# A decoder block on one core: the first adaLN vectors through TensorE, six blocks in step, constants loaded after them

## The chip, the core and the metric

The kernel runs on one core of one Trainium2 chip. The metric is device microseconds for one execution of the whole program, from the profiler's side the span from the first to the last instruction plus a little around it. Before the change three runs took 2737.02, 2737.36 and 2742.2 us; the median, 2737.36 us, is the time that a change is compared with. Engines are named as the profile names them: PE is the matrix engine, PEld its weight loads, DVE the vector engine, ACT the scalar engine, POOL GpSimd, SP the engine that issues all the DMAs here.

## The reference

One decoder layer, batch 1, 2048 tokens, width 1024, all float32. A condition vector gives six vectors of 1024; the first two shift and scale the input of the token-mixing sub-layer, the others come later:

```python
cond = jax.nn.silu(c)
mod = (cond @ w_ada[l] + b_ada[l])[:, None, :]
sh1, sc1, g1, sh2, sc2, g2 = jnp.split(mod, N_MOD, axis=-1)
h = rms_norm(x, norm1_g[l]) * (1 + sc1) + sh1
proj = h @ w_in[l]
gq, gk, gv, gr, glr, aq, ak, av = jnp.split(proj, split_at, axis=-1)
# gated linear attention on the first five, dilated attention on the last three
x = x + g1 * (mixed @ w_out[l])
h = rms_norm(x, norm2_g[l]) * (1 + sc2) + sh2
u = causal_depthwise_conv(h @ w_up[l], conv_w[l], conv_b[l])
x = x + g2 * ((jax.nn.silu(u_gate) * u_val) @ w_down[l])
```

`w_ada` is 1024 x 6144 floats, 25 MB: 48 row blocks of 128 outputs, 512 KB each. Blocks 0 to 7 give sh1 and 8 to 15 sc1.

## The kernel before

Tokens go through in four chunks of 512, channels on the partitions. A float32 product is made of three matmuls in a faster format: each operand is split into a high part (a cast on ACT, `hhi` for activations, `whi` for weights) and the remainder (a subtraction on DVE, or on POOL where `pool=True`: `hlo`, `wlo`), and `mm3` adds high x high, high x low and low x high into PSUM. A weight block is loaded into one of two `wraw` buffers and split into one of three `whi`/`wlo` pairs (`wslot`, `wblock`).

**The start** (`run`, up to `self.consts()`). `ada_setup` loads the condition, broadcast over the partitions, and makes the SiLU; `load_x` loads chunk 0; `norm_stats` makes the RMS factor. Then a loop over the eight channel blocks k: `ada(8 + k)` and `ada(k)` load two 512 KB row blocks of `w_ada` (already transposed, so that the outputs lie on the partitions), and DVE multiplies each with the broadcast condition and sums along the row in one instruction (`tensor_tensor_reduce`, in the profile CUSTOM_DVE_ANT_0, line 281). `norm_mod1` then scales and shifts block k of x (line 331 on DVE, 333 on ACT, 335 on DVE) into `hhi` and `hlo`. Four blocks of the input projection (`FIRST`, 128 columns of `w_ch` each) have their weights ready and take each k as it comes.

**After the start** `consts()` loads the constant tables, masks, convolution weights and norm gains; only the table itself waits (`after`) for the seventh turn of the loop (`GATE`), the other loads go as early as the scheduler puts them. The rest of the 32 row blocks of `w_ada` (g1, sc2, sh2, g2) follow one after another through ONE buffer (`tag="v4", bufs=1`): the load of the next can be issued only when DVE has finished with the one before. In program order these 32 steps are laid along the 52 steps of the input projections (`along` in `run`). `proj(0)` finishes chunk 0: four blocks gq, gk out of the four that `FIRST` has made, then the token-major blocks (`tok`, 272 or 256 columns, x as the stationary operand) and the eight q and k blocks (`qk`); `begin(1)` prepares chunk 1's `hhi` and `hlo`, whose squares are summed by `norm_stats` before.

**What sets the order.** The program text gives the order of dependencies; a scheduler then places every instruction on its engine by its own model of durations. Each engine, and SP for the loads, works its list strictly from the top. From the second quarter of the list on, the lists of before and of the change are nearly the same; they differ at the start.

## Time and profile before

| | before |
|---|---|
| median of 3 runs | 2737.36 us |
| profiled execution, its time | 2739.4 us |
| its span, mean granted clock | 2737.6 us, 0.978 |
| PE busy over the span | 2622.8 us (96%) |
| DVE, ACT, POOL busy | 1889.6, 1265.5, 518.8 us |
| bytes moved | 405.19 MB |

The profiled execution took 2.0 us more than the median of the runs. Busy PE does not mean PE at its peak, because matmuls overlap: a matmul's record lasts about 0.39 us where the next starts 0.23 us behind it. Rows of the timeline give the start (us from the span's start), the duration, the engine, the line, the operation and its operands; what stands in square brackets is the idle time before and what ended it.

### The profile page before, as it was taken

The numbers are of one execution on the slowest core, as the hardware profiler recorded it, in microseconds if no ns is written. First come the engines' busy times: TensorE is split into PE (matmuls) and PEld (weight loads), VectorE is DVE, ScalarE is ACT, GpSimd is POOL, SyncE is SP. The second block draws the span as 40 slices with busy tenths as digits, with TensorE's granted clock in tenths as the row PEclk, the third lists the DMA queues.
The fourth block names the chain that finished last, engine by engine and source line by source line (L and its number), as shares of the span: only waits on it lengthen the run. The fifth ranks groups of instructions, "written<-read, shape, count | busy, mean of one in ns | idle before, by whom it ended". The sixth has DMA issues, their size and how long they took to land.

```text
span 2737.6 us, 48297 instructions
## 1 busy us (share of the span) xinstructions
PE 2622.8 (96%) x18920; PEld 2172.7 (79%) x18920; DVE 1889.6 (69%) x3740; ACT 1265.5 (46%) x2606; POOL 518.8 (19%) x324
## 2 busy tenths in 40 slices
PE   5989999999979999999999999999999999999999
PEld 4978888888858887778777888887777788788887
DVE  8777575555567776667987677778877667575655
ACT  3555456465435444443544444435444444343332
POOL 1233242222222211100230111013111100011110
PEclk9999999999979999999999999999999999999999
DMA  7877454554632333336434444544443435333232
GB/s 276 289 260 243 145 186 154 195 173 147 197 113 93 99 123 122 106 122 232 137 97 124 130 136 126 169 168 128 130 129 113 140 122 187 125 100 100 93 100 93
DMA packets 196230, 405.19 MB, mean 148 GB/s; under 512 B 19474, under 2 KB 78627, under 8 KB 194723
## 3 DMA queue, kind: packets, MB, share of 16 engines
q1 hardware_dynamic: 196002, 402.11, 45.1%
q8 instruction: 149, 2.44, 0.4%
q14 instruction: 79, 0.64, 0.1%
HBM read 339.12 MB, written 62.91 MB: 147 GB/s over the span
## 4 chain that ended last, share of the span: by engine, by line
PE 66%; DVE 14%; ACT 9%; DMA 7%; issue 3%; SPq 1%; POOL 0%; DVEq 0%; ACTq 0%; POOLq 0%
PE psg L239 19%; PE psg L241 19%; PE psg L240 19%; DMA wada<-in_w_ada_dram 3%; ACT big L641 3%; DVE wlo L224 2%; PE psa L722 2%; PE psa L631 2%; PE psa L751 2%; ACT whi L223 1%; ACT s L641 1%; DVE big L637 1%; DMA sq<-in_xT_dram 1%; DVE wada L281 1%; DVE y L819 1%
## 5 line engine op out<-in xcount | busy, mean ns | idle before, releaser
L239 PE MATMUL psg<-hhi,whi 128*128 128x512 f32 x2040 | 818.5, 403 | 21.9 <-ACT hhi L333 10.4
L241 PE MATMUL psg<-hhi,wlo 128*128 128x512 f32 x2040 | 808.8, 397 | 10.6 <-DVE wlo L224 10.5
L240 PE MATMUL psg<-hlo,whi 128*128 128x512 f32 x2040 | 808.4, 397 | 7.2 <-DVE hlo L335 7.1
L223 ACT CAST whi<-wraw 128x1024 fp32r<-128x1024 f32 x391 | 408.6, 1049 | 573.9 <-PE psg L240 400.5
L224 DVE TENSOR_TENSOR wlo<-wraw,whi 128x1024 fp32r<-128x1024 f32 (+1 forms) x300 | 393.8, 1313 | 188.4 <-ACT whi L223 177.1
L224 POOL TENSOR_TENSOR wlo<-wraw,whi 128x1024 fp32r<-128x1024 f32 x91 | 225.6, 2479 | 1392.7 <-ACT whi L223 1169.3
L239 PEld LDWEIGHTS psg<-hhi,whi 128*128 128x128 f32 x2040 | 390.1, 191 | 115.9 <-ACT hhi L333 13.9
L241 PEld LDWEIGHTS psg<-hhi,wlo 128*128 128x128 f32 x2040 | 389.4, 191 | 96.2 <-DVE wlo L224 13.9
L240 PEld LDWEIGHTS psg<-hlo,whi 128*128 128x128 f32 x2040 | 390.3, 191 | 89.5 <-DVE hlo L335 10.8
L239 PE MATMUL psg<-ghi,whi 128*128 128x512 f32 x704 | 279.3, 397 | 0.0
L240 PE MATMUL psg<-glo,whi 128*128 128x512 f32 x704 | 277.1, 394 | 0.0
L241 PE MATMUL psg<-ghi,wlo 128*128 128x512 f32 x704 | 274.4, 391 | 0.0
L863 DVE SCALAR_TENSOR_TENSOR x<-psg,mod,x 128x512 f32<-128x512 f32 x192 | 143.0, 748 | 159.2 <-PE psg L241 154.8
L239 PE MATMUL psg<-whi,hhi 128*128 128x256 f32 (+1 forms) x768 | 222.5, 292 | 7.9 <-DVE stg L422 3.9
L241 PE MATMUL psg<-whi,hlo 128*128 128x256 f32 (+1 forms) x768 | 222.1, 292 | 5.6 <-DVE hlo L335 5.6
L240 PE MATMUL psg<-wlo,hhi 128*128 128x256 f32 (+1 forms) x768 | 221.4, 290 | 0.4 <-DVE wlo L224 0.4
L819 DVE SCALAR_TENSOR_TENSOR y<-psg,conv_w_sb,y 128x511 f32<-128x511 f32 x176 | 130.9, 744 | 94.1 <-ACT y L818 93.5
L239 PEld LDWEIGHTS psg<-whi,hhi 128*128 128x128 f32 x768 | 149.8, 196 | 12.4 <-issue 3.7
L239 PEld LDWEIGHTS psg<-ghi,whi 128*128 128x128 f32 x704 | 132.2, 188 | 33.1 <-issue 5.4
L241 PEld LDWEIGHTS psg<-whi,hlo 128*128 128x128 f32 x768 | 149.8, 196 | 8.5 <-DVE hlo L335 6.8
L240 PEld LDWEIGHTS psg<-glo,whi 128*128 128x128 f32 x704 | 132.3, 188 | 28.8 <-issue 3.1
L241 PEld LDWEIGHTS psg<-ghi,wlo 128*128 128x128 f32 x704 | 132.2, 188 | 27.9 <-DVE wlo L224 0.6
(198 smaller groups left out, 3672.9 us busy)
## 6 DMA issues: line engine op xcount, KB each, us to landing
wraw<-in_w_up_dram SPq DMA_DIRECT2D x176, 512.0 KB, 3.4
wraw<-in_w_down_dram SPq DMA_DIRECT2D x88, 512.0 KB, 3.4
wraw<-in_w_ch_dram SPq DMA_DIRECT2D x48, 512.0 KB, 4.0
wada<-in_w_ada_dram SPq DMA_DIRECT2D x40, 512.0 KB, 5.0
wraw<-in_w_tok_dram SPq DMA_DIRECT2D x40, 512.0 KB, 4.0
v<-v SPq DMA_DIRECT2D x68, 256.0 KB, 5.1
wraw<-in_w_out_dram SPq DMA_DIRECT2D x32, 512.0 KB, 4.0
sq<-in_xT_dram SPq DMA_DIRECT2D x48, 256.0 KB, 3.7
```

The source lines that it names most:

```text
L223: nc.scalar.copy(hi[:, :n], raw[:, :n])
L224: (nc.gpsimd if pool else nc.vector).tensor_tensor(lo[:, :n], raw[:, :n], hi[:, :n].bitcast(F32), op=ALU.subtract)
L239: nc.tensor.matmul(ps, wh, hh, start=first and k == 0, stop=False, skip_group_check=shared)
L240: nc.tensor.matmul(ps, wh, hl, start=False, stop=False, skip_group_check=shared)
L241: nc.tensor.matmul(ps, wl, hh, start=False, stop=k == n - 1, skip_group_check=shared)
L281: self.last = nc.vector.tensor_tensor_reduce(raw, raw, self.cond[:, i * n:(i + 1) * n], 0.5, m if i else 0.0, ALU.mult, ALU.add, m)
L631: nc.tensor.matmul(at(i, hh, z), q[H[hh], i * P:(i + 1) * P], key(H[hh], i, z), start=True, stop=True, skip_group_check=True)
L641: nc.scalar.activation(t[:, lo:hi], t[:, lo:hi], AF.Exp, bias=nm[:, hh, g, i:i + 1], scale=2.0 ** -(h + 1), accum_out=dn[:, hh, g, i:i + 1])
L722: nc.tensor.transpose(ps[:n, i * P:(i + 1) * P], part(S[hh], i), self.C("id"))
L751: nc.tensor.matmul(out, lhsT, rhs, start=first[hh], stop=False, skip_group_check=True)
L819: nc.vector.scalar_tensor_tensor(y[:, 1:], ps[:, :T - 1], self.cw[:, 1, b:b + 1], y[:, 1:], op0=ALU.mult, op1=ALU.add)
L863: nc.vector.scalar_tensor_tensor(x1, ps, self.mod[:, 40 + cb:41 + cb], x1, op0=ALU.mult, op1=ALU.add)
```

## The change

- `sh1` and `sc1` no longer come from DVE. `w_ada1` holds the first 2048 columns of `w_ada` in another layout: four groups u of 512 columns, 256 of sc and 256 of sh, so that group u gives both vectors for channel blocks 2u and 2u + 1. `ada_first(u)` loads 2 MB and runs eight float32 matmuls with the condition, replicated to 32 columns (`crep`), as the stationary operand; matmul k writes PSUM partitions 32j to 32j + 31 with j = k mod 4. ACT copies the result, and four small matmuls against a vector of 1/64 (`sel`) sum the four strips and the replicas and turn the row into a column. Two small DVE instructions add the bias and form the gain.
- The pieces of groups 0 and 2 go through the four `big` buffers, those of 1 and 3 through eight buffers that are used later for other things (`y0`, `y1`, `stage`, `s16`).
- Six blocks of `w_ch` instead of four are carried along: the fourth and fifth have their split weights in `kt`, the sixth in `gp` buffers, in two halves; the last two accumulate in `psa` banks. `FIRST` therefore also covers `qk(0)` and `qk(1)`, and `proj(0)` runs these before `tok(0)`.
- All loads of `consts()` now wait for one instruction: the addition of the bias in group u = 2.

```diff
-GATE = 6
-FIRST = (0, 1, 2, 3)
+FIRST = (0, 1, 2, 3, 4, 5)
...
+    def gated(self, out, in_):
+        self.after(self.nc.sync.dma_start(out, in_))
...
-        self.mk = self.cload("masks", MASKS.shape, U32)
+        self.gated(self.ct, A["consts"])
+        self.mk = self.cload("masks", MASKS.shape, U32, True)
...
+    def ada_first(self, u):
+        nc = self.nc
+        ps = self.pa()
+        raws = []
+        for i in range(4):
+            src = self.A["w_ada1"][u, i]
+            if u % 2:
+                pool, tag = ((self.up, "y0"), (self.up, "y1"), (self.at, "stage"), (self.at, "s16"))[i]
+                for j in range(2):
+                    raws.append(pool.tile([P, T], F32, name="wada", tag=tag, bufs=2))
+                    nc.sync.dma_start(raws[-1], src[:, j * T:(j + 1) * T])
+            else:
+                raw = self.at.tile([P, 1024], F32, name="wada", tag="big", bufs=4)
+                nc.sync.dma_start(raw, src)
+                raws += [raw[:, 0:T], raw[:, T:]]
+        for k in range(KD):
+            j = k % 4
+            nc.tensor.matmul(ps[32 * j:32 * j + 32], self.crep[:, k], raws[k], start=k < 4, stop=k >= 4, skip_group_check=True)
+        t = self.tmp.tile([P, T], F32, name="sq", bufs=3)
+        nc.scalar.copy(t, ps)
+        pm = self.pa()
+        for i in range(4):
+            nc.tensor.matmul(pm[:, i:i + 1], t[:, i * P:(i + 1) * P], self.sel, start=True, stop=True, skip_group_check=True)
+        v = lambda t: t.rearrange("p (a k) -> p a k", a=2)
+        two = slice(2 * u, 2 * u + 2)
+        self.gate_ins = nc.vector.tensor_tensor(v(self.mod[:, 0:16])[:, :, two], v(pm[:, 0:4]), v(self.ba[:, 0:16])[:, :, two], op=ALU.add)
+        nc.vector.scalar_tensor_tensor(self.G1[:, two], self.mod[:, 8 + 2 * u:10 + 2 * u], 1.0, self.n1[:, two], op0=ALU.add, op1=ALU.mult)
...
-        for k in range(KD):
-            big = [self.at.tile([P, 1024], F32, name="wada", tag="big", bufs=4)]
...
-            h0.append(self.norm_mod1(xs[k], k, rstd[0], self.G1, self.mod[:, 0:8]))
-        for b in FIRST:
-            for k in range(KD):
-                self.mm3(done[b], ws[b][k:k + 1], h0[k:k + 1], k == 0, True)
+        for u in range(4):
+            self.ada_first(u)
+            for b in {0: (0, 1, 2), 1: (3, 4), 2: (5,)}.get(u, ()):
+                src = self.A["w_ch"][b]
+                if b < 5:
+                    ws[b] = self.wblock(src, KD, P, b % 2 == 1, slot(b))
+                else:
+                    ws[b] = []
+                    for i, part in enumerate(slot(b)):
+                        ws[b] += self.wblock(src[:, i * T:(i + 1) * T], 4, P, True, part)
+            if u == 2:
+                gate = self.gate_ins
+            for k in (2 * u, 2 * u + 1):
+                h0.append(self.norm_mod1(xs[k], k, rstd[0], self.G1, self.mod[:, 0:8]))
+            for b in ws:
+                for k in range(at.get(b, 0), 2 * u + 2):
+                    self.mm3(done[b], ws[b][k:k + 1], h0[k:k + 1], k == 0, True)
+                at[b] = 2 * u + 2
+        self.gate_ins = gate
         self.consts()
...
-            yield from chain(glaqk(0), glaqk(1), glaqk(2), glaqk(3), tok(0), qk(0), qk(1), tok(1), qk(2), ...
+            yield from chain(glaqk(0), glaqk(1), glaqk(2), glaqk(3), qk(0), qk(1), tok(0), tok(1), qk(2), ...
```

Line numbers below of the changed program are its own: the matmuls of `ada_first` are L313 and L318 there, `mm3` is L242 to L244, the bias addition L321, the gain L322, `norm_mod1` L367 and L371, the reduction of a `w_ada` block L288, the remainder `wlo` L227.

**Third group on PE.** The list of the changed program's PE where the eight matmuls of group u = 2 (into `psa_392`) stand. `w0_330` and `w0_335` are the split weights of the fourth and fifth block of `w_ch`.

```order
L244 MATMUL psg_221<-hhi_346,w0_330 128x512
L242 MATMUL psa_222<-hhi_269,w0_335 128x512
L243 MATMUL psa_222<-hlo_271,w0_335 128x512
L313 MATMUL psa_392<-wada_393,crep_111 32x512 x2
L313 MATMUL psa_392<-wada_395,crep_111 32x512 x2
L313 MATMUL psa_392<-wada_397,crep_111 32x512 x2
L313 MATMUL psa_392<-wada_399,crep_111 32x512 x2
L244 MATMUL psa_222<-hhi_269,w0_335 128x512
```

The matmuls of group 2 stand behind all the work that the fourth block can do with channel blocks 0 to 3, and behind the first two matmuls of the fifth block.

**Last group on DVE.** The list of the changed program's DVE after the constants. `wada_616` and `wada_644` are the second and third of the 32 row blocks that go through one buffer (the first, `wada_606`, stands four rows ahead of the fence); `mod_117<-psa_515` is the bias addition of group u = 3; `x_184` and `x_186` are channel blocks 6 and 7.

```order
L288 ISA wada_616,mod_117<-wada_616,cond_95 128x1024
L288 ISA mod_117 128x1
L289 TENSOR_TENSOR mod_117<-mod_117,b_ada_sb_101 128x1
L352 TENSOR_TENSOR rstd_1009<-rstd_1009,sq_1011 128x512
L321 TENSOR_TENSOR mod_117<-psa_515,b_ada_sb_101 128x2x2
L322 SCALAR_TENSOR_TENSOR G1_118<-mod_117,norm1_g_sb_97 128x2
L367 SCALAR_TENSOR_TENSOR x_184<-x_184,G1_118,rstd_215 128x512
L367 SCALAR_TENSOR_TENSOR x_186<-x_186,G1_118,rstd_215 128x512
L288 ISA wada_644,mod_117<-wada_644,cond_95 128x1024
L288 ISA mod_117 128x1
L371 SCALAR_TENSOR_TENSOR hlo_525<-x_184,mod_117,hhi_523 128x512
L371 SCALAR_TENSOR_TENSOR hlo_530<-x_186,mod_117,hhi_528 128x512
```

Two of the 32 row blocks, and chunk 1's first square, now stand ahead of the last group's bias addition; a third stands ahead of the `hlo` of its channel blocks, and the fourth and fifth ahead of the first `wlo` of `tok(0)`. In the list of before one row block stands ahead of that `wlo`.

**Chunk 1 on DVE.** The list of before, where the first `hlo` of chunk 1 that PE waits for are made. `wada_2224` and `wada_2290` are the 21st and 22nd of the 32 row blocks.

```order
L281 ISA wada_2224,mod_109<-wada_2224,cond_93 128x1024
L281 ISA mod_109 128x1
L335 SCALAR_TENSOR_TENSOR hlo_1813<-sq_1808,mod_109,hhi_1811 128x512
L282 TENSOR_TENSOR mod_109<-mod_109,b_ada_sb_99 128x1
L335 SCALAR_TENSOR_TENSOR hlo_1820<-sq_1815,mod_109,hhi_1818 128x512
L335 SCALAR_TENSOR_TENSOR hlo_1827<-sq_1822,mod_109,hhi_1825 128x512
L224 TENSOR_TENSOR wlo_1883<-wraw_1880,whi_1882 128x1088
L281 ISA wada_2290,mod_109<-wada_2290,cond_93 128x1024
```

And the same place in the changed program, where `wada_2948` and `wada_2971` are the 26th and 27th:

```order
L288 ISA wada_2948,mod_117<-wada_2948,cond_95 128x1024
L288 ISA mod_117 128x1
L371 SCALAR_TENSOR_TENSOR hlo_1861<-sq_1856,mod_117,hhi_1859 128x512
L289 TENSOR_TENSOR mod_117<-mod_117,b_ada_sb_101 128x1
L371 SCALAR_TENSOR_TENSOR hlo_1868<-sq_1863,mod_117,hhi_1866 128x512
L371 SCALAR_TENSOR_TENSOR hlo_1875<-sq_1870,mod_117,hhi_1873 128x512
L227 TENSOR_TENSOR wlo_1931<-wraw_1928,whi_1930 128x1088
L288 ISA wada_2971,mod_117<-wada_2971,cond_95 128x1024
```

The work itself stands in the same order; five more row blocks are ahead of it. Behind it ten row blocks are left in the list of before, five in that of the change.

More of the change, by code (lines that the diff above doesn't have):

```diff
@@ L245, in ada_setup @@
         nc, c = self.nc, self.A["c"]
+        cc = self.cload("c_col", [P, KD])
         self.cond = self.const.tile([P, 1024], F32, name="cond")
@@ L254, in ada_setup @@
         nc.vector.memset(self.eps, EPS)
+        self.sel = self.const.tile([P, 1], F32, name="sel")
+        nc.vector.memset(self.sel, 1.0 / 64)
+        tc_ = self.const.tile([P, KD], F32, name="tcol")
+        nc.scalar.activation(tc_, cc, AF.Tanh, scale=0.5)
+        self.crep = self.const.tile([P, KD, 32], F32, name="crep")
+        rep = lambda t: t[:, :, None].to_broadcast([P, KD, 32])
+        nc.vector.scalar_tensor_tensor(self.crep, rep(tc_), 1.0, rep(cc), op0=ALU.add, op1=ALU.mult)
         th = self.at.tile([P, 1024], F32, name="big", bufs=4)
@@ L266, in after, with ada @@
         self.tc.add_manual_dep(inst.ins, self.gate_ins.ins.name, mybir.DependencyInfo(mybir.DependencyClass.Sync, mybir.DependencyReason.DATA))
-    def ada(self, b, raws=None):
+    def ada(self, b):
         nc = self.nc
-        if raws is None:
-            raws = [self.at.tile([P, 1024], F32, name="wada", tag="v4", bufs=1)]
-        n = 1024 // len(raws)
-        for i, raw in enumerate(raws):
-            ld = nc.sync.dma_start(raw, self.A["w_ada"][b][:, i * n:(i + 1) * n])
-            if b == 16:
-                self.after(ld)
+        raw = self.at.tile([P, 1024], F32, name="wada", tag="v4", bufs=1)
+        ld = nc.sync.dma_start(raw, self.A["w_ada"][b - 16])
+        if b == 16:
+            self.after(ld)
@@ L278, in ada @@
         yield
         m = self.mod[:, b:b + 1]
-        for i, raw in enumerate(raws):
-            self.last = nc.vector.tensor_tensor_reduce(raw, raw, self.cond[:, i * n:(i + 1) * n], 0.5, m if i else 0.0, ALU.mult, ALU.add, m)
+        nc.vector.tensor_tensor_reduce(raw, raw, self.cond, 0.5, 0.0, ALU.mult, ALU.add, m)
         nc.vector.tensor_tensor(m, m, self.ba[:, b:b + 1], op=ALU.add)
-        for j, G, g in ((1, self.G1, self.n1), (4, self.G2, self.n2)):
-            if b // KD == j:
-                k = b % KD
-                nc.vector.scalar_tensor_tensor(G[:, k:k + 1], m, 1.0, g[:, k:k + 1], op0=ALU.add, op1=ALU.mult)
+        if b // KD == 4:
+            k = b % KD
+            nc.vector.scalar_tensor_tensor(self.G2[:, k:k + 1], m, 1.0, self.n2[:, k:k + 1], op0=ALU.add, op1=ALU.mult)
@@ L440, in proj @@
         if done:
-            yield from chain(glaqk(0), glaqk(1), glaqk(2), glaqk(3), tok(0), qk(0), qk(1), tok(1), qk(2), qk(3), tok(4), qk(4), tok(5), qk(5), qk(6), tok(2), qk(7), tok(3))
+            yield from chain(glaqk(0), glaqk(1), glaqk(2), glaqk(3), qk(0), qk(1), tok(0), tok(1), qk(2), qk(3), tok(4), qk(4), tok(5), qk(5), qk(6), tok(2), qk(7), tok(3))
         else:
@@ L894, in run, with slot @@
-        for b in FIRST:
-            for k in range(KD):
-                self.mm3(done[b], ws[b][k:k + 1], h0[k:k + 1], k == 0, True)
+        h0, ws, at, done = [], {}, {}, {b: self.pg() if b < 4 else self.pa() for b in FIRST}
+        def slot(b):
+            if b < 3:
+                return None
+            if b < 5:
+                t = self.at.tile([P, 2048], F32R, name="w0", tag="kt", bufs=2)
+                return t[:, 0:1024], t[:, 1024:2048]
+            return [(self.gp.tile([P, T], F32R, name="whi", tag="ghi"), self.gp.tile([P, T], F32R, name="wlo", tag="glo")) for _ in range(2)]
```

39 lines of the change are left out of this document (13 added, 26 removed).

## The prediction

> **What bounds the kernel now.** I read the page's busy shares first, then the span cut into stages, then the chain and the waits of the first 200 us, because only the list's start is changed.
>
> ```profile
> PE 2622.8 (96%) x18920; PEld 2172.7 (79%) x18920; DVE 1889.6 (69%) x3740; ACT 1265.5 (46%) x2606; POOL 518.8 (19%) x324
> 0.00:62.00 62.00, 32.14 (x100) 21.69 (x100) 52.33 (x105) 21.90 (x30) 10.96 (x10) 0.94 0.77 273
> 62.00:192.00 130.00, 124.68 (x821) 113.77 (x821) 90.84 (x134) 69.49 (x105) 36.51 (x27) 1.00 0.84 281
> 192.00:262.00 70.00, 62.11 (x599) 52.42 (x598) 57.36 (x86) 40.68 (x72) 30.47 (x23) 0.88 0.77 245
> 262.00:2738.00 2476.00, 2403.87 (x17403) 1984.86 (x17402) 1689.06 (x3419) 1133.43 (x2400) 440.83 (x265) 0.98 0.42 135
> ```
>
> Columns: stage, its length, busy us of PE, PEld, DVE, ACT, POOL, granted clock, DMA share, GB/s. PE is the bound over the whole. Of its idle time the first 62 us hold 62 - 32.1 = 29.9 us, the next 130 us only 5.3, the 70 us after these 7.9 with a clock of 0.88. In the first stage the change's target is plain: DVE is busy 52.3 of 62 us. But between 62 and 192 us something else runs along, and it decides my forecast:
>
> ```profile
> by line: DMA wada<-in_w_ada_dram 52.0%; DVE wada L281 10.9%; issue 8.5%; DMA wraw<-in_w_tok_dram 5.2%; DVE wlo L224 4.0%; DMA sq<-in_xT_dram 4.0%; DMA wraw<-in_w_ch_dram 3.2%; DVE sq L303 1.7%; DVE stg L371 1.6%; ACT whi L223 1.5%; DVE nwt
> L281 DVE CUSTOM_DVE_ANT_0 wada<-wada,cond x21: 1211/1226/2091, 63.3 to 189.9; 128x1024 f32<-128x1024 f32 x21
> L275 SPq DMA_DIRECT2D wada<-in_w_ada_dram x21: 327/333/419, 64.5 to 191.2; - x21
> DMA to landing us min/median/max: 3.2/4.7/6.9
> DVE wada L281 <- DMA wada<-in_w_ada_dram: 24.1, 16, 3.2
> ```
>
> The first row is the chain of waits from 62 to 200 us, the next three the tile `wada` from 62 to 192 us, the last DVE's longest wait there. The 32 row blocks behind the first sixteen go through one buffer: load, reduce, next load. Twenty-one issues from 64.5 to 191.2 us make 20 rounds of 6.3 us; 4.7 us of landing, 1.2 of reduction and a little for the issue make 6.0, so the rounds are back to back, and 63% of that chain is this one buffer. PE hardly feels it, because the splits of the weights run ahead of it in three buffers. It feels it where chunk 1 begins:
>
> ```profile
> 189.95 1.23 DVE L281 CUSTOM_DVE_ANT_0 wada<-wada,cond 128x1024 f32<-128x1024 f32 x1 [1.37 <-DMA wada<-in_w_ada_dram]
> 195.50 0.74 DVE L335 SCALAR_TENSOR_TENSOR hlo<-sq,mod,hhi 128x512 fp32r<-128x512 f32 x1
> 196.29 0.39 PE L241 MATMUL psg<-whi,hlo 128*128 128x272 f32 x1 [1.32 <-DVE hlo L335]
> ```
>
> DVE waits for the 22nd row block, then makes the `hlo`, and PE waits for that.
>
> **The change part by part.** *Removed from DVE:* sixteen reductions of 1.22 us with their small additions, about 22 us of the 52.3. *Added to PE:* four groups of eight float32 matmuls with 32 output columns.
>
> ```profile
> L318 PE MATMUL psa<-rstd,ones 128*128 128x512 f32 x16 | 10.2, 727 | 18.5 <-DVE rstd L316 18.5
> L651 PE MATMUL psa<-kt,qf 64*32 64x128 f32 x256 | 6.3, 272 | 0.0
> L746 PE MATMUL psa<-v,s 128*32 128x64 f32 x256 | 4.4, 221 | 0.0
> L703 PE MATMUL psa<-xm,consts_sb 128*128 128x32 f32 x32 | 4.9, 233 | 0.0
> ```
>
> A float32 matmul has two records. L318, full width, costs 10.2 / 8 = 1.28 us. L651, 32 output columns in four strips as here, costs 6.3 / 128 = 0.049 us for 128 moving columns, so 0.20 for 512, if strips overlap here as there. A group is 1.6 us at the low end and 8 x 1.28 = 10.2 at the high; I take the low, since L746 has the full 128 rows too and is as cheap. Four `sel` matmuls at the 0.15 of a record of L703, two records each, are 1.2 us.
>
> *The start, followed through.* The loads come at this rate (same columns, from 5 us on):
>
> ```profile
> 5.00:10.00 5.00, 0.00 (x0) 0.00 (x0) 3.50 (x5) 4.94 (x8) 0.00 (x0) 1.00 1.03 380
> 10.00:15.00 5.00, 0.58 (x1) 0.50 (x2) 4.69 (x10) 1.43 (x4) 0.00 (x0) 1.00 1.03 401
> 15.00:20.00 5.00, 1.49 (x2) 0.00 (x0) 4.71 (x8) 2.31 (x3) 2.34 (x1) 1.00 1.03 399
> 12.53 1.22 DVE L281 CUSTOM_DVE_ANT_0 wada<-wada,cond 128x1024 f32<-128x1024 f32 x1
> ```
>
> At 400 GB/s, and with the first 3.2 MB usable at 12.5 us, bytes up to B MB are usable at about 12.5 + (B - 3.2) / 0.4, plus 0.4 for the added `c_col` issue. Group 0 (4.8 MB with x ahead of it) is there at 16.9, group 1 (7.9) at 24.7, group 2 (10.0) at 29.9, group 3 (13.2) at 37.9. The pieces wait for their buffers: group 2 for group 0's matmuls (18.7), the second half of group 3 for group 1's (30), both before the queue runs dry, so nothing is lost there. The fifth block lands near 39; the sixth in halves, each waiting for a `wraw` buffer that POOL or DVE must have left:
>
> ```profile
> L223 ACT CAST whi<-wraw x6: 1029/1048/1087, 14.9 to 66.5; 128x1024 fp32r<-128x1024 f32 x4, 128x1088 fp32r<-128x1088 f32 x2
> L224 POOL TENSOR_TENSOR wlo<-wraw,whi x3: 2342/2352/2652, 16.1 to 36.9; 128x1024 fp32r<-128x1024 f32 x3
> 24.12 0.63 PE L240 MATMUL psg<-hlo,whi 128*128 128x512 f32 x1
> 24.55 0.63 PE L239 MATMUL psg<-hhi,whi 128*128 128x512 f32 x1
> 46.01 0.39 PE L240 MATMUL psg<-hlo,whi 128*128 128x512 f32 x1
> 46.23 0.39 PE L241 MATMUL psg<-hhi,wlo 128*128 128x512 f32 x1
> ```
>
> The last half lands at about 44 and is cast by 44.8, ahead of group 2's copy on ACT. On PE group 2's matmuls stand behind the fourth block (36 matmuls at 0.23 us from 34 us, the split on POOL at 38.8) and end near 44.5. Copy 0.6, ten matmuls 2.3, `sel` 1.2: the bias addition of group 2, and with it the constants' release, is at 48 us. The twelve matmuls of the sixth block, group 3 and 36 matmuls (2.7 + 1.6 + 8.2), behind a wait of 0.2, bring PE to 60.6, `sel` to 61.7.
>
> Now what is queued behind the released loads. In before the first row block was issued at 51.3 and used at 58.3:
>
> ```profile
> 51.32 0.43 SPq L275 DMA_DIRECT2D wada<-in_w_ada_dram  x1
> 58.33 1.23 DVE L281 CUSTOM_DVE_ANT_0 wada<-wada,cond 128x1024 f32<-128x1024 f32 x1 [0.18 <-DMA wada<-in_w_ada_dram]
> 62.00 0.39 PE L240 MATMUL psg<-wlo,hhi 128*128 128x272 f32 x1 [0.45 <-DVE wlo L224]
> ```
>
> After, SP issues nine small constant loads first (0.45 us each, 48.2 to 52.3), so the first is used at 56 to 57 with less ahead of it, the second about 62, and only then does DVE reach group 3's bias addition, at 64 instead of 61.9; gain, x and `hhi` (0.15 + 0.7 + 0.7) let PE go on at 65.7, a gap of 4 us. The third row block delays the `hlo` to 68.7, another 1.6. The 30 matmuls left (6.8 us) end at 75.5, but the first `wlo` of `tok(0)` stands behind the fifth row block: 57 + 4 x 5.0 (landing 3.6, little else is loading) = 77, reduced by 78.2, `wlo` by 79.4. Before stood there at 62.0 and had 48 matmuls (two blocks) less behind it, 10.9 us: 72.9. **The start loses 6.5 us**, between 4 (rounds of 4.5) and 10 (rounds of 6).
>
> *The stretch to chunk 1.* PE has 130 - 5.3 - 10.9 = 114 us of work left for what was 62 to 192, and could be at chunk 1 by 193. DVE gets there after the 27th row block instead of the 22nd: 22 rounds from 78. At 6.3 us that is 216; with some 7% fewer bytes a round (two weight blocks and five x tiles have moved forward) I take 5.8, so 205 against 191.1. **PE stands 14 us later here**, the 6.5 included.
>
> *Behind it* five row blocks fewer are left: 5 x 1.4 = 7 us less on DVE, which was busy 57.4 of 70 us. PE's own loss there was 7.9 idle and 0.12 x 70 = 8.4 by the clock; I give half back, 8 us, bounds 0 and 16. From 262 us on the lists agree, and PE bound stays PE bound.
>
> Sum: 14 - 8 = +6, against the profiled 2739.4; that execution was 2.0 above the median, so 2737.4 + 6 = 2743.4, **2743.5 us**.
>
> A gap of 4 us on PE may also bring back the slow spacing (0.43 us at 24.12, 0.23 at 46.01). The Trainium skill, TensorE: Matmul & The Clock Gate, Part 1, has the clock at half after an idle window and full after about 3.4 us of work; by it the gap costs an estimated 1.7 us more and the time would be 2745. The rows above show both spacings, not what switches them.
>
> **The rivals.** *Faster: the buffer's rounds follow PE and do not lead it.* For it: DVE waits only 24.1 us for these loads in 130, and landings of 3.2 us occur. Then 22 rounds fit before PE's 193 at (193 - 78) / 22 = 5.2 us or less; PE is there as early as before, and all the 8 us behind come back: 2737.4 - 8 = 2729.5. Against it: DVE waited for 16 of the 21 loads. The Trainium skill, DMA: Bandwidth & Descriptors, Anatomy of one DMA, gives 2.0 us plus bytes over 436 GB/s (for another issuing path), an estimated 3.2 us for 512 KB: by that rule this rival holds; the trace agrees in its minimum, 3.2, not in its median, 4.7.
>
> *No change:* rounds of 5.5 give 199 at the 27th, +8 at chunk 1, and the same 8 back: 2737.5.
>
> *Much slower: the strips do not overlap.* Each group is 10.2 instead of 1.6 us on a waiting path; groups 0 and 1 fall partly under loading, group 2 delays the constants by 8.6, group 3 PE itself: some 12 us more, 2755. It decides from about 4 us for a group's eight matmuls. Against it: L651 and L746. *That the change does not unload the start* is excluded as to DVE, whose reductions are gone from the list; it could still be that loading alone set the start.
>
> **How the numbers follow.** Forecast (rounds 5.6 to 6.3, 2740 to 2752) 0.40, no change 0.25, faster 0.25, strips 0.10. About 0.2%, 5.5 us, is what a measurement of this kernel can tell. Slower by more: 0.32 of the forecast's 0.40, 0.03 of the middle case, all 0.10, so 0.45; faster: 0.22 + 0.02 = 0.24; the same 0.31. The range 2728 to 2757 leaves out the far ends of the outer cases; the likeliest case's own is 2740 to 2752.
>
> **What would show it.** The eight L313 matmuls of a group within 1.6 to 3.4 us: strips overlap. Group 2's bias addition at 45 to 51 us; PE idle about 4 us ahead of the first matmuls of blocks 6 and 7, released by ACT `hhi`; `wlo` of `tok(0)` behind a DVE wait for `wada`. Then the round length: 205 us at the 27th row block. Rounds of 5.2 or a start ready before 73 us would make the prediction wrong.

## The result, and the profile after

The changed kernel takes **2756.3 us** (median of 4 runs, 2753.9 to 2761.2) beside 2737.2 us of the kernel before (4 runs). The ratio is 1.0069, with a 95% interval of 1.0049 to 1.0090: 19 us slower. The forecast was 2743.5 us, with a range of 2728 to 2757. The profiled execution shown below took 2753.91 us, its span is 2752.1, so against the profiled execution of before the span grew by 14.5 us, less than the medians did; the traces account for 14.5 of the 19 us.

The page's busy shares and the stages, columns as in the prediction:

```profile
PE 2636.8 (96%) x19016; PEld 2178.5 (79%) x19016; DVE 1865.3 (68%) x3685; ACT 1269.4 (46%) x2612; POOL 515.3 (19%) x324
0.00:62.00 62.00, 43.19 (x190) 25.13 (x191) 23.94 (x40) 22.43 (x31) 9.01 (x10) 0.97 0.75 266
62.00:192.00 130.00, 108.96 (x658) 97.57 (x657) 81.77 (x130) 55.49 (x89) 28.46 (x18) 0.91 0.76 251
```

The change does what it says: in the first 62 us DVE is busy 23.9 us instead of 52.3, PE 43.2 instead of 32.1. The price shows in the second row. PE, busy 124.7 of 130 us before at a clock of 1.00, is busy 109.0 us at 0.91. What PE waits for there stands in three places of the timelines of DVE, SP and PE:

```profile
50.91 0.16 DVE L321 TENSOR_TENSOR mod<-psa,b_ada_sb 128x4 f32<-128x4 f32 x1 [8.74 <-PE psa L318]
55.20 0.41 SPq L155 DMA_DIRECT2D gB<-in_gla_norm_g_dram  x1
64.33 0.43 DVE L195 TENSOR_SCALAR gB<-gB 128x512 f32<-128x512 f32 x1 [7.94 <-DMA gB<-in_gla_norm_g_dram]
65.55 1.23 DVE L288 CUSTOM_DVE_ANT_0 wada<-wada,cond 128x1024 f32<-128x1024 f32 x1 [0.79 <-DMA wada<-in_w_ada_dram]
72.51 0.16 DVE L321 TENSOR_TENSOR mod<-psa,b_ada_sb 128x4 f32<-128x4 f32 x1
...
74.45 1.65 PE L242 MATMUL psg<-hhi,whi 128*128 128x512 f32 x3 [9.64 <-ACT hhi L369]
86.87 0.39 PE L243 MATMUL psg<-wlo,hhi 128*128 128x272 f32 x1 [1.11 <-DVE wlo L227]
103.01 0.50 PE L399 MATMUL psa<-sqr,blk 128*128 128x512 f32 x1 [2.81 <-POOL sqr L393]
105.29 0.38 PE L485 MATMUL psa<-consts_sb,gl 128*16 128x128 f32 x1 [1.78 <-ACT gl L454]
115.27 1.99 PE L492 MATMUL psa<-gw,glr 17*128 17x256 f32 x8 [1.24 <-DVE glr L488]
```

First place: `gB`, the gain of the gated attention's norm, is one of the constants that now wait for group 2's addition (50.9 us). Its load is issued at 55.2 us; DVE waits 7.94 us for it, then works off two row blocks, and only at 72.5 does it add the bias of the last group. PE, out of work at 64.8, waits 9.64 us for what follows from that. Second place: `tok(0)`'s first low part is used at 86.9 us. In the kernel before that was at 62.0, with 10.9 us of matmuls (blocks 4 and 5) still to come that the change has done by then. On equal work it is 72.9, so the change is 14 us late. Third place: from 100 to 115 us PE waits three times more, for the norm of `qk(1)` (L399) and the gate of `tok(0)` (L485, L492), where the kernel before had no wait at all. The granted clock follows:

```profile
62.00:96.00 34.00, 34.00 (x223) 30.87 (x224) 22.08 (x33) 21.38 (x38) 2.12 (x2) 1.00 0.92 322
96.00:126.00 30.00, 30.00 (x192) 27.01 (x191) 21.25 (x32) 15.82 (x25) 12.93 (x8) 1.00 0.86 285
```

is the kernel before, and

```profile
62.00:96.00 34.00, 23.25 (x124) 20.06 (x124) 19.97 (x36) 13.64 (x21) 1.28 (x1) 0.80 0.71 233
96.00:126.00 30.00, 24.03 (x145) 22.05 (x144) 19.59 (x30) 13.91 (x28) 9.64 (x5) 0.83 0.72 248
```

the changed one. Two landmarks behind that (PE's first wait in chunk 1, for the high part of its fourth channel block, and SP's first load of `w_out`), of before and then of the change:

```profile
193.32 0.39 PE L239 MATMUL psg<-whi,hhi 128*128 128x272 f32 x1 [1.19 <-ACT hhi L333]
701.85 0.33 SPq L217 DMA_DIRECT2D wraw<-in_w_out_dram  x1
```

```profile
221.74 0.39 PE L242 MATMUL psg<-whi,hhi 128*128 128x272 f32 x1 [2.08 <-ACT hhi L369]
721.69 0.33 SPq L220 DMA_DIRECT2D wraw<-in_w_out_dram  x1
```

The change is 14.0 us late at `tok(0)`, 28.4 at chunk 1, 19.8 at `w_out`, 14.6 at the first of SP's last four loads of `w_up` (at 2659.8 before, 2674.4 now), 14.5 at the end. So the start costs 14 us, the stretch to chunk 1 another 14, and about as much comes back behind it. Of the second 14, PE's gaps between `tok(0)` and chunk 1 make 7.7 (14.2 us in all against 6.5, added up from its timeline); the other 6.7 are about what the lower clock costs there: the mean granted clock from `tok(0)` to chunk 1 is 0.95 over 134.9 us, 1.00 before, an estimated 6.7 us.

### The profile page after: what moved, and what is told of

Same layout as the page of the kernel before. It is cut to its first block, busy times and chain, and to the rows that moved or that the text cites. A ratio compares the mean times of both kernels' runs of the same rounds, so it can differ in the third digit from the quotient of the medians.

```text
span 2752.1 us, 48456 instructions
## 1 busy us (share of the span) xinstructions
PE 2636.8 (96%) x19016; PEld 2178.5 (79%) x19016; DVE 1865.3 (68%) x3685; ACT 1269.4 (46%) x2612; POOL 515.3 (19%) x324
## 4 chain that ended last, share of the span: by engine, by line
PE 70%; DVE 12%; ACT 9%; DMA 6%; issue 3%; POOL 0%; SPq 0%; DVEq 0%; ACTq 0%; POOLq 0%
PE psg L242 20%; PE psg L244 20%; PE psg L243 20%; ACT big L677 3%; DMA wada<-in_w_ada_dram 3%; PE psa L758 2%; PE psa L667 2%; PE psa L787 2%; DVE wlo L227 2%; ACT whi L226 1%; ACT s L677 1%; DMA sq<-in_xT_dram 1%; DVE big L673 1%; DVE y L855 1%; PE psa L536 1%
## 5 line engine op out<-in xcount | busy, mean ns | idle before, releaser
L242 PE MATMUL psg<-hhi,whi 128*128 128x512 f32 x2024 | 811.5, 403 | 22.6 <-ACT hhi L369 14.7
L244 PE MATMUL psg<-hhi,wlo 128*128 128x512 f32 x2024 | 801.2, 397 | 10.3 <-DVE wlo L227 10.2
L227 DVE TENSOR_TENSOR wlo<-wraw,whi 128x1024 fp32r<-128x1024 f32 (+1 forms) x300 | 392.0, 1307 | 188.9 <-ACT whi L226 172.7
L227 POOL TENSOR_TENSOR wlo<-wraw,whi 128x1024 fp32r<-128x1024 f32 (+1 forms) x91 | 222.3, 2443 | 1384.8 <-ACT whi L226 1135.4
L242 PEld LDWEIGHTS psg<-hhi,whi 128*128 128x128 f32 x2024 | 386.2, 191 | 114.7 <-ACT hhi L369 16.7
L244 PEld LDWEIGHTS psg<-hhi,wlo 128*128 128x128 f32 x2024 | 385.9, 191 | 95.9 <-DVE wlo L227 14.4
L242 PE MATMUL psg<-ghi,whi 128*128 128x512 f32 x704 | 279.2, 397 | 0.0
L244 PE MATMUL psg<-ghi,wlo 128*128 128x512 f32 x704 | 274.4, 391 | 0.0
L242 PE MATMUL psg<-whi,hhi 128*128 128x256 f32 (+1 forms) x768 | 224.3, 294 | 7.1 <-ACT hhi L369 4.6
L244 PE MATMUL psg<-whi,hlo 128*128 128x256 f32 (+1 forms) x768 | 222.6, 292 | 3.7 <-DVE hlo L371 3.7
L242 PEld LDWEIGHTS psg<-whi,hhi 128*128 128x128 f32 x768 | 151.1, 197 | 11.1 <-ACT hhi L369 5.1
L242 PEld LDWEIGHTS psg<-ghi,whi 128*128 128x128 f32 x704 | 132.1, 188 | 33.1 <-issue 4.9
L244 PEld LDWEIGHTS psg<-whi,hlo 128*128 128x128 f32 x768 | 150.8, 197 | 6.2 <-DVE hlo L371 4.4
L244 PEld LDWEIGHTS psg<-ghi,wlo 128*128 128x128 f32 x704 | 132.2, 188 | 28.0 <-DVE wlo L227 0.6
```

Source lines behind the costliest of these rows:

```text
L227: (nc.gpsimd if pool else nc.vector).tensor_tensor(lo[:, :n], raw[:, :n], hi[:, :n].bitcast(F32), op=ALU.subtract)
L242: nc.tensor.matmul(ps, wh, hh, start=first and k == 0, stop=False, skip_group_check=shared)
L244: nc.tensor.matmul(ps, wl, hh, start=False, stop=k == n - 1, skip_group_check=shared)
```

## The experiments

Twelve kernels were run, each beside the kernel before on the same chip. The ratio to that kernel is the yardstick; the changed kernel stands at 1.0069.

| run | us | kernel before | ratio, 95% interval |
|---|---|---|---|
| plain `gB` | 2747.4 | 2736.0 | 1.0050, 1.0034 to 1.0067 |
| constants early | 2758.3 | 2736.0 | 1.0084, 1.0070 to 1.0098 |
| row blocks late | 2754.3 | 2736.0 | 1.0073, 1.0060 to 1.0086 |
| second row-block buffer | 2754.5 | 2736.0 | 1.0070, 1.0057 to 1.0084 |
| cover by order | 2752.2 | 2734.3 | 1.0058, 1.0042 to 1.0074 |
| four blocks | 2744.0 | 2734.3 | 1.0033, 1.0022 to 1.0045 |
| plain `gB`, hold | 2749.8 | 2734.3 | 1.0056, 1.0042 to 1.0069 |
| plain `gB`, hold, cover by order | 2745.2 | 2734.3 | 1.0042, 1.0027 to 1.0057 |
| four blocks, plain `gB` | 2738.6 | 2732.9 | 1.0019, 1.0009 to 1.0029 |
| four blocks, plain `gB`, hold | 2745.8 | 2732.9 | 1.0046, 1.0033 to 1.0059 |
| plain `gB`, hold, matmuls doubled | 2753.4 | 2732.9 | 1.0073, 1.0061 to 1.0085 |
| four blocks, plain `gB`, last group first | 2730.0 | 2735.4 | 0.9978, 0.9968 to 0.9988 |

**Plain `gB`.**

```diff
-        self.gated(self.gB, bass.AP(tensor=g.tensor, offset=g.offset, ap=[[0, P], [0, 4], [1, P]]))
+        self.gated(self.gB, A["gla_norm_g"])    # laid out on the host for every partition, [P, 4, P]
```

> The changed kernel with one load altered: the table gB (256 KB) comes from a copy that the host lays out for every partition, in one plain piece of 2 KB a partition, instead of one row of 128 numbers read over and over by a broadcast pattern; it stays behind the gate. Theory A (the broadcast load itself is slow and holds up what stands behind it on its queues and on VectorE): gB arrives about 5 us after its issue at 55.2 instead of 9.1, VectorE's wait of 7.94 us ahead of its scaling falls to about 4, the first row block is used at 60 to 62 instead of 65.55, the last group's addition comes at 67 to 69 instead of 72.51, the first low part of tok(0) at about 82 to 83 instead of 86.87; the rounds keep their 6.1 us, so chunk 1's first hlo comes at 219 to 220 instead of 223.92, and the time falls by about 4 us, 2752. Theory B (the wait is only that loads issued late meet other traffic): gB takes as long, nothing moves, 2756. Theory C (the added matmuls and the work in step cost the time, not this queue): the stage up to tok(0) may shorten, the time stays 2756.

The list of DMA issues from 0 to 70 us (bytes each, median time to landing), of the changed kernel:

```profile
gB<-in_gla_norm_g_dram SPq DMA_DIRECT2D x1, 256.0 KB, 9.1
cond<-in_c_dram SPq DMA_DIRECT2D x1, 512.0 KB, 3.9
```

and of this run, with its timeline of DVE and PE:

```profile
gB<-in_gla_norm_g_dram SPq DMA_DIRECT2D x1, 256.0 KB, 2.7
57.48 0.43 DVE L194 TENSOR_SCALAR gB<-gB 128x512 f32<-128x512 f32 x1 [1.52 <-DMA gB<-in_gla_norm_g_dram]
59.30 1.23 DVE L287 CUSTOM_DVE_ANT_0 wada<-wada,cond 128x1024 f32<-128x1024 f32 x1 [1.40 <-DMA wada<-in_w_ada_dram]
66.03 0.15 DVE L320 TENSOR_TENSOR mod<-psa,b_ada_sb 128x4 f32<-128x4 f32 x1
67.97 1.65 PE L241 MATMUL psg<-hhi,whi 128*128 128x512 f32 x3 [3.91 <-ACT hhi L368]
80.13 0.39 PE L242 MATMUL psg<-wlo,hhi 128*128 128x272 f32 x1 [1.45 <-DVE wlo L226]
215.00 0.39 PE L241 MATMUL psg<-whi,hhi 128*128 128x272 f32 x1 [2.26 <-ACT hhi L368]
```

The same 256 KB at the same place land in 2.7 us instead of 9.1, the first row block is used 6.3 us earlier, PE's gap is 3.9 us instead of 9.6, and `tok(0)`'s first low part comes at 80.1 instead of 86.9. The time is 11.4 us above the kernel before, where the changed kernel is 19.1; the two intervals overlap, so the gain in time is less sure than its place. The place is plain: 6.7 us earlier at `tok(0)`, 6.7 at PE's first wait in chunk 1 (215.0 instead of 221.7, the last row), 7.7 at the end of the profiled execution. Theory A holds, with more gain than it gave. Theory B falls: the late issue is not what made the load slow (it is as slow in the kernel before, 9.3 us, issued at 27.7). Theory C falls as far as the start goes; from `tok(0)` to chunk 1 this run takes 134.9 us, as the change does, so the second loss is another one. The Trainium skill, DMA: Bandwidth & Descriptors, Anatomy of one DMA, gives 2.0 us plus bytes over 436 GB/s (for another issuing path), an estimated 2.6 us for 256 KB; the plain load agrees, the broadcast one does not.

**Constants early, row blocks late.** The first leaves only the constants table behind the gate; the second holds the first row block until the last group's addition:

```diff
-        self.mk = self.cload("masks", MASKS.shape, U32, True)      # and the same for the other constants
+        self.mk = self.cload("masks", MASKS.shape, U32)
```

> The changed kernel with only the first table of constants behind the gate, as in the kernel before; masks, convolution weights, norm gains, the gate's matrix and gB are loaded unheld, early. Theory A (the held constants delay the row blocks and hold VectorE): the gate stays near 50.9 or comes a little later because their bytes stand among the matrix pieces; the first row block is issued about 51 to 52 and used at 57, the last group's addition at 65, the first low part of tok(0) at 79 to 80 instead of 86.87, the 27th row block 22 rounds of 6.1 later, 210 instead of 218.4, the time 2748 (8 us less). Theory C (work in step and added matmuls cost it): PE's idle time of 9.6 us at 64.8 shrinks but the time stays 2756. A mishap that is possible: the scaling of gB now stands ahead of group 1's addition on VectorE and gB's slow load delays that addition; then the gate comes at 55 or later and nothing is gained.

```diff
+            if u == 3:
+                self.last = self.gate_ins
...
         if b == 16:
-            self.after(ld)
+            # the same dependency, on self.last
```

> The changed kernel with the first row block held until the last group's bias addition instead of the third's; the constants stay where they are. No row block then stands ahead of the last group's addition on VectorE (two did), three instead of four or five ahead of tok(0)'s first low part, about 25 instead of 27 ahead of chunk 1. Theory A (two separate losses: the start, by the row blocks ahead of the last group and of tok(0), and chunk 1, by the number of rounds): the last group's addition comes at about 65 to 66 (only gB's wait is left ahead of it), the PE gap of 9.6 us shrinks to about 3, tok(0)'s first low part at 82 to 84; the chain starts about 10 us later, so chunk 1's hlo stays at 220 to 224, and the time stays within 3 us of 2756. Theory C (chunk 1's delay follows from the start's delay): the start gains 4 to 7 us and the time falls by as much, 2750.

DVE's timeline of the first run, then of the second:

```profile
36.48 0.43 DVE L195 TENSOR_SCALAR gB<-gB 128x512 f32<-128x512 f32 x1 [9.60 <-DMA gB<-in_gla_norm_g_dram]
36.82 0.15 DVE L321 TENSOR_TENSOR mod<-psa,b_ada_sb 128x4 f32<-128x4 f32 x1
56.13 0.16 DVE L321 TENSOR_TENSOR mod<-psa,b_ada_sb 128x4 f32<-128x4 f32 x1 [5.54 <-PE psa L318]
```

```profile
70.92 0.69 DVE L352 TENSOR_TENSOR rstd<-rstd,sq 128x512 f32<-128x512 f32 x1 [3.12 <-ACT sq L347]
74.76 0.15 DVE L321 TENSOR_TENSOR mod<-psa,b_ada_sb 128x4 f32<-128x4 f32 x1
```

Neither helps: in both, an instruction that waits still stands ahead of an addition on DVE's list, only another one or another addition. Loaded early, `gB` stalls DVE for 9.6 us ahead of group 1's addition, so the gate opens at 56.1 instead of 50.9 (the mishap that was named). With the row blocks held, chunk 1's statistics (L352, whose x tiles SP loads next) move ahead of the last group's addition and make it later still, 74.8. The hold of the second run was thus not the clean test of the row blocks that it was meant to be.

**A second buffer for the row blocks.**

```diff
-        raw = self.at.tile([P, 1024], F32, name="wada", tag="v4", bufs=1)
+        if b % 2:
+            raws = [self.gp.tile([P, T], F32, name="wada", tag=t) for t in ("ghi", "glo")]
```

> The changed kernel with a second buffer for every second row block (two halves in a pair of idle tiles), so that two loads are under way at once. In the list seven row blocks then stand ahead of tok(0)'s first low part and all 32 ahead of chunk 1. Theory A (the chain load, reduce, load through one buffer sets chunk 1's start): two blocks come in 6 to 7 us, all 32 are reduced by 175 to 185, chunk 1's first hlo follows PE and comes at about 197 to 203 instead of 223.92; tok(0) stays near 87; no row blocks are left behind chunk 1, and the time falls by 18 to 25 us, to 2731 to 2738. Theory C (the chain is not what binds; PE's 14 us of added busy time are): chunk 1 stays near 220, the time within 4 us of 2756. Theory D (the transfers share a fixed rate): the rounds of a pair stay at 12 us, nothing moves.

The time is 18.4 us above the kernel before, so there is no gain; but the run did not do what was intended. The tile `wada` from 62 to 225 us has 16 whole reductions, and 8 that end a pair of halves:

```profile
L294 DVE CUSTOM_DVE_ANT_0 wada<-wada,cond x26: 679/1224/1756, 66.3 to 222.9; 128x1024 f32<-128x1024 f32 x16, 128x512 f32<-128x512 f32 x10
L294 DVE CUSTOM_DVE_ANT_0 wada<-wada,cond,mod x8: 737/750/1145, 68.2 to 203.4; 128x512 f32<-128x512 f32 x8
```

These are 24 row blocks by then, when all 32 were expected by 185. The pair shares its tiles with the norms of `qk`, which may be why its loads came late; that was not tested. The run decides nothing about the chain.

**Cover by order, and four blocks.** The waits at 100 to 115 us could come from the six blocks in step: they use up in the start the matmuls of `qk(0)` and `qk(1)`, which lay behind `tok(0)` before and hid its gate. One run puts other blocks there, one goes back to four:

```diff
-... qk(0), qk(1), tok(0), tok(1), qk(2), qk(3), tok(4) ...
+... qk(0), qk(1), tok(0), qk(2), qk(3), tok(1), tok(4) ...
```

> The changed kernel with one change in the order in which work is handed out behind the start: qk(2) and qk(3) come ahead of tok(1) instead of behind it, so that two blocks of matmuls (10.9 us) lie between tok(0) and tok(1), as qk(0) and qk(1) did in the kernel before. Theory K (the six blocks in step use up, in the start, the two blocks of matmuls that hid tok(0)'s gate and the norm of qk(0); the PE gaps of 2.8, 1.8 and 1.2 us from 100 to 115 us in the changed kernel, and the lower clock from 96 to 126 us behind them, come from that): these gaps go or shrink to under 2 us in all, the clock there is back at about 1.0, tok(1) to tok(5) come 8 to 10 us earlier, and the time falls by 6 to 10 us, to 2746 to 2750. Theory R (the row blocks' chain sets chunk 1's start): the gaps go, chunk 1 still waits until about 218 to 222, and the time stays within 3 us of 2756.

```diff
-FIRST = (0, 1, 2, 3, 4, 5)
+FIRST = (0, 1, 2, 3)
...
-... glaqk(3), qk(0), qk(1), tok(0), tok(1) ...
+... glaqk(3), tok(0), qk(0), qk(1), tok(1) ...
```

> The changed kernel with only four blocks in step in the start, and tok(0) ahead of qk(0) and qk(1) as before: the matmul form of shift and scale, the three sets of buffers and the held constants stay. Theory K (six blocks in step take the cover from tok(0)'s gate): PE has two blocks less in the start, so its gap ahead of the last group's matmuls grows from 9.6 to about 10 to 14 us (gB and the row blocks release it as before), but the 10.9 us of qk(0) and qk(1) come back as cover behind tok(0): the gaps at 100 to 115 us are gone, the time is 2746 to 2752. Theory S (six blocks fill PE's waiting time in the start and are worth their 10 us): the time rises to 2760 to 2766.

PE in the run with the other order, then the stages, `tok(0)` and the first wait in chunk 1 of the run with four:

```profile
103.20 0.79 PE L399 MATMUL psa<-sqr,blk 128*128 128x512 f32 x1 [2.90 <-POOL sqr L393]
105.77 0.38 PE L485 MATMUL psa<-consts_sb,gl 128*16 128x128 f32 x1 [1.77 <-ACT gl L454]
```

```profile
62.00:96.00 34.00, 30.66 (x160) 27.00 (x159) 19.02 (x30) 15.56 (x29) 0.83 (x1) 0.86 0.90 295
96.00:126.00 30.00, 30.00 (x182) 26.54 (x182) 20.52 (x33) 16.21 (x25) 8.59 (x7) 1.00 0.75 246
72.69 0.59 PE L243 MATMUL psg<-wlo,hhi 128*128 128x272 f32 x1 [0.24 <-DVE wlo L227]
208.75 0.40 PE L242 MATMUL psg<-whi,hhi 128*128 128x272 f32 x1 [1.84 <-ACT hhi L369]
```

The other order left two of the three waits where they were, because PE's list has the blocks behind them; neither K's gain nor R's time can be read from it, and its ratio cannot be told from the change's. With four blocks they are gone: PE is busy all 30 us from 96 to 126 at a clock of 1.00, and the time is 9.8 us above the kernel before instead of 19.1. Part of that is the start: 72.7 plus the 10.9 us still to come is 83.6 on equal work, 3.3 better than the change. The larger part is the cover: from `tok(0)` to that wait PE takes 136.1 us, 125.2 on equal work, where the change and the run with plain `gB` take 134.9 and the kernel before 131.3, or 120.4 on equal work. Theory S falls. Theory K holds behind `tok(0)`; for the start it had PE's gap grow to 10 to 14 us, and the gap was 4.0, because group 2's addition comes at 36.5 us instead of 50.9 and `gB` is issued at 42.4 instead of 55.2.

**The start mended piece by piece, with six blocks.** The hold makes the row blocks and chunk 1's statistics loads wait for the start's last `hlo`:

```diff
         self.consts()
+        self.gate_ins = self.hlo_ins     # later uses of after(): row block 16, chunk 1's first x loads
```

> The changed kernel with gB in the plain layout, and the first row block and chunk 1's first statistics loads held until the last hlo of the start, so that nothing of either stands ahead of the last group's addition on VectorE. Theory A (the start's remaining loss is what stands there): against the run with plain gB alone, the PE gap of 3.9 us ahead of the last group's matmuls falls to about 1 to 2, tok(0)'s first low part comes at 75 to 78 instead of 80.1, and the time is 2741 to 2745. Theory R (the row blocks' chain sets chunk 1's start): the chain starts 11 us later, so chunk 1 comes as late or later than in that run (217), and the time is 2747 or more.

> All three at once: gB plain, row blocks and statistics loads held until the last hlo of the start, qk(2) and qk(3) ahead of tok(1). Theory A with K (the start's wait on VectorE, then the lost cover, each on PE's path): the time is 2733 to 2738, at or below the kernel before. Theory C (the added 14 us of busy time on PE are the price and are not won back): 2742 or more even with both gaps gone.

With plain `gB` and hold the gap is 1.99 us and `tok(0)`'s first low part comes at 78.5 instead of 80.1, a little behind the 75 to 78 expected, yet the time is not better than with plain `gB` alone. Theory R gave that time (2747 or more), but not for its reason: chunk 1's fourth `hlo` comes at 214.0 instead of 217.2, so what is gained by then is lost behind it. With the other order as well it is 2745.2 us, 10.9 above the kernel before, where A with K gave 2733 to 2738. Theory C gave 2742 or more, but with the gaps gone, and PE's wait for the gate is still there, 6.0 us from 96, so the run decides nothing between them. The hold was then tried on the better base, with four blocks:

> Four blocks in step and tok(0) ahead of qk(0) and qk(1) (the run with four, 9.8 us slower than the kernel before), and gB in the plain layout (the run with plain gB, 11.4 us slower). Theory A with K (gB's wait on VectorE and the lost cover are two separate losses of about 8 and 10 us that add up): 2735 to 2739, level with the kernel before. Theory P (with four blocks the last group's matmuls stand behind the blocks' in PE's queue until 55.7 us, so gB's wait, over at 52, is already covered there; PE's added float32 matmuls hold the start): the time falls by under 3 us against the run with four, 2742 to 2745, and tok(0)'s first low part stays at 70 to 73 us.

> The same with the row blocks and chunk 1's statistics loads held until the last hlo of the start. Theory A: the last group's addition follows PE within 0.5 us instead of 2, no row block stands between the two hlo, PE's gap of 4.0 us falls to about 2, and the time is 2 to 4 us below the run without the hold. Theory H (held loads only arrive later: as in the run that held them with six blocks, what the start gains is lost behind it): no gain, within 2 us of the run without the hold.

Four blocks with plain `gB` take 2738.6 us. That lies in the 2735 to 2739 of A with K, but those were to be level with the kernel before, which on this chip takes 2732.9, 5.7 less; the interval excludes level. `tok(0)`'s first low part stays at 73.0, as P said, so the step from the run with four was not won at `tok(0)`. The intervals of these two overlap, and whether and where something was won stays open. The hold costs 7 us here, with intervals that don't touch. The last reduction of a row block, without and with it:

```profile
251.06 1.31 DVE L287 CUSTOM_DVE_ANT_0 wada<-wada,cond 128x1024 f32<-128x1024 f32 x1
```

```profile
269.67 1.21 DVE L287 CUSTOM_DVE_ANT_0 wada<-wada,cond 128x1024 f32<-128x1024 f32 x1
```

Chunk 1's fourth `hlo` comes at the same time in both (209.9 and 209.7), but with 26 row blocks done in the one and 23 in the other. Three row blocks more are left to the stretch behind it, and the end comes 7 us later. Theory A falls; H is right that there is no gain, but it gave 2 us at most, and that the row blocks make the 7 us is argued, not separated.

**The added matmuls by themselves.**

```diff
-        for k in range(KD):
+        for k in 2 * tuple(range(KD)):
```

> The run with plain gB and held row blocks (six blocks; 15.5 us slower than the kernel before), with the eight float32 matmuls of each of the four groups issued twice, the second pass writing over the first: 32 matmuls more, 2 to 3 us of PE a group. Theory P (the start is bound by PE, so the added matmuls are paid for in full from the second group on): tok(0)'s first low part comes 5 to 8 us later than in that run (78.5), and the time rises by 5 to 8 us, to 2754 to 2758. Theory V (VectorE and the loads set the start, PE has room): tok(0) and the time move by under 2 us.

```profile
42.13 3.63 PE L312 MATMUL psa<-wada,crep 128*32 128x512 f32 x30
53.76 3.62 PE L312 MATMUL psa<-wada,crep 128*32 128x512 f32 x26
82.76 0.39 PE L242 MATMUL psg<-wlo,hhi 128*128 128x272 f32 x1 [0.95 <-DVE wlo L226]
```

The matmuls of groups 2 and 3 take 3.6 us each doubled, 1.9 before: 3.4 us more in all. `tok(0)` comes 4.2 us later than in the run it is compared with (82.8 against 78.5). The time is 3.6 us longer (4.6 by the ratios), but the two intervals overlap. The place is nearer to P than to V, though less than P gave: once `gB` is plain and the row blocks are held, PE's own work from group 2 on sets when `tok(0)` starts, and what is put on it is paid there.

**The last group first.** Then the order of that work should matter. With four blocks the last group's matmuls are strewn among the blocks' and end behind them. PE's last of the eight, and what follows on DVE and PE in that run:

```profile
57.47 1.04 PE L312 MATMUL psa<-wada,crep 128*32 128x512 f32 x2
60.33 0.16 DVE L320 TENSOR_TENSOR mod<-psa,b_ada_sb 128x4 f32<-128x4 f32 x1 [5.67 <-PE psa L317]
62.28 1.65 PE L241 MATMUL psg<-hhi,whi 128*128 128x512 f32 x3 [1.99 <-ACT hhi L368]
63.73 0.63 PE L241 MATMUL psg<-hhi,w 128*128 128x512 f32 x1
64.16 0.63 PE L242 MATMUL psg<-hlo,whi 128*128 128x512 f32 x1
72.99 0.39 PE L242 MATMUL psg<-wlo,hhi 128*128 128x272 f32 x1 [0.44 <-DVE wlo L226]
```

The edit calls `ada_first(3)` ahead of the blocks' matmuls of k 4 and 5, and ties two places down:

```diff
+            if k == 0 and u == 3:        # the eight together, behind the group's last load
+                ... first matmul after ld
...
+            if u == 2:
+                self.ada_first(3)
+                self.behind = self.sel_mm    # the blocks' matmuls of k 4 and 5 behind its sel
```

> Four blocks in step and plain gB (the run that is 5.7 us slower than the kernel before), with one change in PE's order: the last group's eight float32 matmuls are issued together, behind the last of its loads, and it and its sel stand ahead of the blocks' matmuls of k 4 and 5 instead of being strewn singly among them and ending behind them. Theory P (PE sets the start: a lone float32 matmul of 32 columns costs 1.05 us and eight together 1.9, the last group's addition at 60.3 us holds the final 24 matmuls, which then run at half clock): the eight take 1.9 us, the addition comes at 49 to 53, PE's idle time of 2.0 us at 60.3 and the slow matmuls behind it (24 in 8.3 us instead of 5.6) go, tok(0)'s first low part comes at 63 to 66 instead of 73, and the time falls by 6 to 10 us, to 2729 to 2733, below the kernel before. Theory V (the start is set by VectorE and its waits for row blocks, wherever PE's matmuls stand): tok(0) comes 3 us earlier at most, and the time stays at 2736 to 2739.

```profile
42.26 1.92 PE L315 MATMUL psa<-wada,crep 128*32 128x512 f32 x16
47.54 0.16 DVE L325 TENSOR_TENSOR mod<-psa,b_ada_sb 128x4 f32<-128x4 f32 x1 [1.17 <-PE psa L322]
59.24 0.39 PE L245 MATMUL psg<-wlo,hhi 128*128 128x272 f32 x1
62.00:192.00 130.00, 125.38 (x820) 114.59 (x818) 94.69 (x133) 69.39 (x104) 40.12 (x27) 0.99 0.82 271
```

The eight take 1.9 us in one piece, the addition comes at 47.5 instead of 60.3, `tok(0)`'s first low part at 59.2 instead of 73.0, and PE is busy 125.4 of 130 us at 0.99 in the second stage, as in the kernel before. The kernel takes 2730.0 us, ratio 0.9978 (0.9968 to 0.9988): 5 us faster than the kernel before, and by the ratios about 25 us faster than the change. P holds, with more won at `tok(0)` than it gave; V falls. Against the run with four blocks and plain `gB` only this order differs, with what the scheduler moved along with it: two row blocks that stood ahead of the last group's addition on DVE now stand behind it. They are not what held it there, since DVE's wait ahead of it, 5.67 us, was for PE.

## Why the prediction was right, and where it was not

Slower was right, and so was half of the place: a start that gets late between group 2's addition and `tok(0)`. The size was 13 us short: 6 us were forecast and 19 measured. That 2756.3 still lies inside the range is luck. It is 0.7 us from the end; the forecast's own case reached to 2752, and the part of the range above it stood for strips that do not overlap (2755), which did not happen.

- *Strips overlap.* Held. The eight of groups 2 and 3 take 1.92 us against the 1.6 that was taken; the rival of 10.2 us falls. Group 0's eight took 3.2 us (16.2 to 19.4), at a granted clock of 1.00 in the profile's rows, so why stays open, and part of group 1's ran singly at 1.05. The bias addition of group 2 came at 50.9 instead of 48.
- *First row block used at 56 to 57, the second at 62.* **This step failed.** The first row block was used at 65.55. The nine constant loads were counted as issues of 0.45 us; what they take to land was not. `gB` takes 9.1 us, and its scaling stands in DVE's list ahead of the first row block. This could have been read before the result: in the kernel before the same load takes 9.3 us, where nothing waits for it. With plain `gB` the chain of times reads 59.3, 66.0 (64 predicted), a gap of 3.9 us (4 predicted), `tok(0)` at 80.1 (79.4 predicted). So the steps behind it nearly hold once this one term is mended; that `tok(0)` fits better than the first row block is two misses that cancel, a start 2.3 us late and four rounds of 4.6 us instead of 5.0.
- *The start loses 6.5 us.* It lost 14.0; with plain `gB` 80.1 - 72.9 = 7.2.
- *The gap may bring back the slow spacing.* It did; the estimate of 1.7 us, by the Trainium skill, TensorE: Matmul & The Clock Gate, Part 1, was left out of the sum. The 36 matmuls behind the gap took 11.2 us (74.45 to 85.64) where 0.23 us each would be 8.3: about 2.9.
- *PE has 114 us of work left and could be at chunk 1 by 193; 22 rounds of 5.8 bring DVE there at 205.* **The second step that failed.** DVE used the 27th row block at 218.4:

```profile
84.38 1.23 DVE L288 CUSTOM_DVE_ANT_0 wada<-wada,cond 128x1024 f32<-128x1024 f32 x1 [0.23 <-DMA wada<-in_w_ada_dram]
218.38 1.23 DVE L288 CUSTOM_DVE_ANT_0 wada<-wada,cond 128x1024 f32<-128x1024 f32 x1 [2.25 <-DMA wada<-in_w_ada_dram]
```

  These are 22 rounds of 6.1 us from 84.4: the predicted round was 0.3 us too short, 6.4 us over the 22, and the chain started 6.4 late. But PE did not stand idle until then. Its first matmul of chunk 1, which waits for nothing, came at 216.5 (188.9 before), its last ahead of the first wait ended at 219.7, and at chunk 1's first four waits it lost 5.8 us against 4.9 before. It was late by its own work, its short gaps and its clock: for the 114 us of work it took 132.8. What was missed is the cover: the prediction counted `qk(0)` and `qk(1)` as 10.9 us of work moved forward and at nothing beyond that, and did not name the work that they hid. The run with four blocks shows that the waits behind `tok(0)` go with the fifth and sixth block, and 9.7 of the 14.4 us of that stretch. Whether the single buffer would bind with 27 row blocks ahead of chunk 1 and PE early was not settled, since the second buffer did not fill. In the last run, with 23 ahead, PE came to chunk 1 at 186.7 and lost 3.25 us there to an `hlo`; DVE had then worked for 17 us without a wait, so there it was DVE's own list and not the load.
- *Five row blocks fewer behind chunk 1, 8 us back.* More came back: 28.4 us late at chunk 1, 19.8 at `w_out`, so 8.6, and another 5.2 by the last `w_up` loads. That it is the row blocks that give it back was not tested; the hold with four blocks, three row blocks more behind and 7 us more at the end, agrees in kind. These 13.8 us are the other reason why the time stayed inside the range.
- *Rivals.* No change and faster fall with the round of 6.1 us and `tok(0)` at 86.9. None named what the last run shows: shift and scale by matmuls do pay, by 5 us, with four blocks in step, a plain `gB` and the last group ahead of the blocks' matmuls.

## What to carry to other kernels

When loads are moved behind a gate, look up what each takes to land, not only to issue, and what stands behind its first consumer in that engine's list; a slow load that nothing waited for has no price in the old profile's waits, only in its list of issues. Work that is moved forward to fill a gap also uncovers whatever it hid where it stood: name that chain before the move. And when reductions go from one engine to the one that is the bound, the order on the new engine can decide the sign: here the same matmuls, in one piece and ahead of the blocks' instead of strewn among them, made 1.0019 into 0.9978.
